# A hybrid decoder layer on one core: mLSTM row sums formed by matmuls against a two-column constant, with factors turned through DRAM and key sums taken by VectorE

## The chip, the cores and the metric

The kernel is one launch on one core of a Trainium2 chip. The core has five engines that run side by side and wait for one another through semaphores: PE (TensorE, matrix products; PEld is its weight loads), DVE (VectorE), ACT (ScalarE), POOL (GpSimd) and SP (SyncE, which here issues nearly all DMAs). Each engine works its instructions off in a fixed order, so an instruction that waits holds up all that stand behind it on its engine. The metric is the device time of the launch in microseconds (us), the median of several runs.

## The reference

The layer has 1024 tokens of width 1024: two groups of heads side by side (4 mLSTM heads of width 128, 8 attention heads), an output product, a cross attention, an MLP and norms. The change lies in the mLSTM heads. What they compute, cut from the reference:

```python
scores = jnp.einsum('bhtd,bhsd->bhts', qc, kc) * jnp.exp(dmat - m_t[..., None])
num = (jnp.einsum('bhts,bhsd->bhtd', scores, vc)
       + inter[..., None] * jnp.einsum('bhed,bhtd->bhte', C, qc))
den = scores.sum(-1) + inter * jnp.einsum('bhd,bhtd->bht', n, qc)
h = num / jnp.maximum(jnp.abs(den), jnp.exp(-m_t))[..., None]
...
C_new = decay[..., None, None] * C + jnp.einsum('bhs,bhse,bhsd->bhed', wa, vc, kc)
n_new = decay[..., None] * n + jnp.einsum('bhs,bhsd->bhd', wa, kc)
...
mh = mh * lax.rsqrt(jnp.mean(mh * mh, axis=-1, keepdims=True) + EPS)
mh = mh * ml_norm[l].astype(jnp.float32).reshape(ML_HEADS, ML_DH)
ml_out = (mh.reshape(B, S, ML_W) * jax.nn.sigmoid(ml_o.astype(jnp.float32))).astype(x.dtype)
```

So each head needs, for each token, a sum over the scores (`den`), a sum of squares of `num` over the head's 128 values, and for the second half of the sequence a matrix `C` and a vector `n` carried over from the first half.

## The kernel before

**Tiling.** Tokens lie along the free axis in two halves of 512 (`TH`); the 128 values of a head lie on the partitions. Products that need float32 accuracy are three matmuls of split operands (`mm3`, L186 to L188): `split` (L134, L135) lets ACT copy a value into a shortened type (`hi`) and DVE subtract that from the value (`lo`).

**The mLSTM stage** runs from about 85 to 366 us. For head 0 to 3, `ml_project` makes the keys (`conv_silu`: a product, a convolution over 1024-wide rows on DVE, a SiLU), one tile of attention queries and one of attention keys (`fx_project(0)`, `fx_project(1)`, which have nothing to do with the mLSTM head), the carried state (`carried`), the mLSTM queries (`conv_silu` again), the carried part of numerator and denominator (`carry`) and the output gate `og`. `ml_head` then works over two halves of tokens: for each of four blocks of keys a score product into an `sc` bank, times an exponential (ACT L587, POOL L589, DVE L590), split (L134, L135), and multiplied by the values into the bank `ov`; POOL adds the weighted scores up into `acc` (L594).

**Row sums before.** At the end of a half, `sum_cols` (L217) multiplies each 128-column piece of `acc` and of the squares `sq` by a column of ones: 8 matmuls of one column, whose results lie with tokens on the partitions, 128x4 each. Small DVE operations on 128x8 columns (L612 to L618, with a power on POOL, L204) form the factor `fac`. `to_row` (L249 to L253) transposes `fac` on PE, stores it to DRAM (`facd`) and loads it back as a row spread over 128 partitions. In L629, L630, L137, L138 `num` is multiplied by norm, factor and gate, split and stored to `mix`.

**The carried state before.** `carried` transposes the first half of the keys (L527), scales the transposed columns by a weight `wc` (L529, into `kw`), splits, multiplies by the values (L540) and sums `kw` over tokens by 4 more matmuls with the column of ones (L542).

**What sets the order.** The program is written as straight code and a generator, `ml_head`, whose tail is resumed from `ml_project` of the next head through `next(closing, None)`, so that the end of a head is issued among the products of the next one. A scheduler then fixes one order per engine when the kernel is built. Buffers come in rings: PSUM has `sc` (3 banks), `tp` (2), `mm`, `m2` and `ov` (1 each); SBUF rings `r_a` to `r_y` hold 512-wide tiles, `r_f` (the numerators) two of them. A matmul into a bank waits until the bank's last reader is done, and a write to an `r_` tile waits for the store of the tile that had the buffer before.

## Time and profile before

| | |
|---|---|
| time, median of 3 runs | 1522.53 us (1522.43 to 1523.9) |
| the profiled execution | 1523.35 us, its span 1521.6 us |
| PE busy | 1502.7 us, 99% of the span |
| DVE, ACT, POOL busy | 1100.3, 727.7, 510.1 us |
| granted TensorE clock | 0.998 over the span |
| mLSTM stage, 85 to 366 us | 281 us, a little under a fifth of the span |

Busy time is what an engine spends in instructions; a row of the timeline gives the start, the length, the engine, the line of the source and the tiles as output<-input. Matmuls are pipelined: a row's length is longer than the distance to the next row's start, and it is the distance from one start to the next that PE's time is made of.

### The profile page before, as it was taken

What the parts mean: (1) busy time and instruction counts of PE and PEld (TensorE: products, weight loads), DVE (VectorE), ACT (ScalarE), POOL (GpSimd) and SP (SyncE); (2) the same over time, 40 slices, a digit from 0 to 9 for tenths busy, and PEclk for the clock granted to TensorE, in tenths of its full rate; (3) what the DMA queues carried; (4) which work ended last, traced back from release to release, by engine and by line L of the source; (5) the groups of instructions that cost most, each with busy time, mean ns of one, the idle gap of its engine ahead of it and who ended that gap; (6) DMA issues with size and microseconds to landing.
All of it is one profiled execution on the core that took longest, in us unless ns stands there. A gap on an engine that the chain in (4) does not pass through costs nothing.

```text
span 1521.6 us, 21977 instructions
## 1 busy us (share of the span) xinstructions
PE 1502.7 (99%) x7694; PEld 1261.5 (83%) x7694; DVE 1100.3 (72%) x1743; ACT 727.7 (48%) x1360; POOL 510.1 (34%) x543
## 2 busy tenths in 40 slices
PE   9999999999999999999999999999999999999997
PEld 9988888889999788888888877778787888888887
DVE  7766676765787786944457989898887667787665
ACT  7324343334687665644443456666664621122124
POOL 1003030413364442511110034544555265663322
PEclk9999999999999999999999999999999999999999
DMA  6322223435888886843344437776678777776623
GB/s 239 109 77 87 98 100 114 135 126 157 246 244 267 260 264 230 300 131 124 119 147 157 153 134 277 247 256 242 222 252 286 291 277 276 276 270 248 239 94 111
DMA packets 122538, 299.86 MB, mean 197 GB/s; under 512 B 13614, under 2 KB 28264, under 8 KB 115516
## 3 DMA queue, kind: packets, MB, share of 16 engines
q1 hardware_dynamic: 122428, 298.46, 57.4%
q8 instruction: 60, 0.98, 0.3%
q14 instruction: 50, 0.41, 0.1%
HBM read 199.60 MB, written 98.81 MB: 196 GB/s over the span
## 4 chain that ended last, share of the span: by engine, by line
PE 93%; DVE 3%; ACT 2%; DMA 1%; issue 1%; SPq 0%; DVEq 0%; POOLq 0%; POOL 0%; ACTq 0%
PE tp L186 8%; PE tp L187 8%; PE tp L188 8%; PE m L186 6%; PE sc L186 6%; PE m L187 6%; PE m L188 6%; PE sc L187 6%; PE sc L188 6%; PE mm L186 6%; PE mm L187 6%; PE mm L188 6%; PE ov L186 2%; PE ov L187 2%; PE ov L188 2%; PE ov L801 2%
## 5 line engine op out<-in xcount | busy, mean ns | idle before, releaser
L186 PE MATMUL tp<-act,wl 128*128 128x512 f32 (+1 forms) x440 | 172.9, 393 | 1.2 <-ACT row L1396 0.7
L187 PE MATMUL tp<-act,wh 128*128 128x512 f32 (+1 forms) x440 | 172.1, 391 | 0.0
L188 PE MATMUL tp<-act,wh 128*128 128x512 f32 (+1 forms) x440 | 171.7, 391 | 0.0
L135 DVE TENSOR_TENSOR wl<-wr,wh 128x1024 fp32r<-128x1024 f32 (+2 forms) x95 | 124.5, 1311 | 22.0 <-ACT wh L134 21.4
L134 ACT ACTIVATE wh<-wr 128x1024 fp32r<-128x1024 f32 (+2 forms) x95 | 95.6, 1007 | 75.9 <-PE tp L188 34.7
L186 PE MATMUL mm<-act,wl 128*128 128x512 f32 (+1 forms) x332 | 127.5, 384 | 0.0
L188 PE MATMUL mm<-act,wh 128*128 128x512 f32 (+1 forms) x332 | 127.3, 383 | 0.0
L187 PE MATMUL mm<-act,wh 128*128 128x512 f32 (+1 forms) x332 | 127.2, 383 | 0.0
L186 PE MATMUL m<-act,wl 128*128 128x512 f32 (+1 forms) x308 | 117.7, 382 | 0.5 <-DVE wl L135 0.5
L188 PE MATMUL m<-act,wh 128*128 128x512 f32 (+1 forms) x308 | 117.7, 382 | 0.0
L187 PE MATMUL m<-act,wh 128*128 128x512 f32 (+1 forms) x308 | 117.5, 381 | 0.0
L186 PEld LDWEIGHTS tp<-act,wl 128*128 128x128 f32 x440 | 82.6, 188 | 20.6 <-ACT row L1396 1.2
L188 PEld LDWEIGHTS tp<-act,wh 128*128 128x128 f32 x440 | 82.6, 188 | 18.9
L187 PEld LDWEIGHTS tp<-act,wh 128*128 128x128 f32 x440 | 82.7, 188 | 18.5
L186 PE MATMUL sc<-act,wl 128*128 128x512 f32 (+1 forms) x248 | 97.0, 391 | 1.0 <-DVE wl L135 1.0
L188 PE MATMUL sc<-act,wh 128*128 128x512 f32 (+1 forms) x248 | 96.7, 390 | 0.0
L187 PE MATMUL sc<-act,wh 128*128 128x512 f32 (+1 forms) x248 | 96.6, 390 | 0.0
L1467 POOL TENSOR_TENSOR z<-wr 128x256 f32<-128x256 f32 x56 | 51.7, 944 | 130.6 <-DMA wr<-w_ff2q 116.8
L134 ACT ACTIVATE wh<-z 128x1024 fp32r<-128x1024 f32 (+1 forms) x54 | 55.5, 1028 | 80.8 <-POOL z L1467 58.4
L135 DVE TENSOR_TENSOR wl<-z,wh 128x1024 fp32r<-128x1024 f32 (+1 forms) x54 | 74.3, 1376 | 7.8 <-ACT wh L134 7.6
L134 ACT ACTIVATE w<-wr 128x768 fp32r<-128x768 f32 (+2 forms) x31 | 25.5, 823 | 106.2 <-PE tp L186 33.7
L188 PEld LDWEIGHTS mm<-act,wh 128*128 128x128 f32 x332 | 62.3, 188 | 12.7
(726 smaller groups left out, 4288.4 us busy)
## 6 DMA issues: line engine op xcount, KB each, us to landing
act<-right SPq DMA_DIRECT2D x49, 1024.0 KB
right<-w SPq DMA_DIRECT2D x56, 256.0 KB
wr<-w_ff2q SPq DMA_DIRECT2D x28, 512.0 KB
right<-r_d SPq DMA_DIRECT2D x49, 256.0 KB
right<-r_e SPq DMA_DIRECT2D x49, 256.0 KB
act<-fqk SPq DMA_DIRECT2D x48, 256.0 KB
wr<-w_in SPq DMA_DIRECT2D x20, 512.0 KB
wr<-w_ff SPq DMA_DIRECT2D x20, 512.0 KB
```

The lines of the kernel that those rows point to most:

```text
L134: s.activation(hi, src, AF.Copy)
L135: return v.tensor_tensor(out=lo, in0=src, in1=hi.bitcast(F32), op=ALU.subtract)
L186: nc.tensor.matmul(ps, w[1], x[0], start=first, stop=False, skip_group_check=more)
L187: nc.tensor.matmul(ps, w[0], x[1], start=False, stop=False, skip_group_check=more)
L188: nc.tensor.matmul(ps, w[0], x[0], start=False, stop=last, skip_group_check=more)
L801: nc.tensor.matmul(self.ov[:, c0:], self.fv[:, self.j], t[:, c0:], start=self.j == 0 and t is self.p[1], stop=self.last and t is self.p[0])
L1467: g.tensor_tensor(out=o, in0=x, in1=y, op=op)
```

## The change

Four parts, with the new line numbers:

1. **Sums by a two-column constant.** `sums(hf)` splits `acc` and the squares into `hi` and `lo` (2 ACT copies, 2 DVE subtractions of 128x512), and multiplies all four by a 128x2 piece of the constant `pick` (L586): columns (1, 0) for `acc`, (0, 1) for the squares. So 4 matmuls of 512 columns fill a 2x512 row in an `sc` bank; ACT copies it out (L588) and SP stores it to `sumd` in DRAM (L589).
2. **Turned through DRAM.** A load of `sumd` in another shape (L627) brings the sums to 128x8 columns. `fac` is stored (L639) and loaded twice as a row (L642), without the transpose on PE. `emc` comes by the same way from a store of `tops` instead of 8 transposes.
3. **Carried keys.** The keys are weighted before the transposes: `rels`, a row in DRAM, is loaded on all partitions (L530), exponentiated, and one `tensor_tensor_reduce` (L532) multiplies and sums for `n_`. The transposes (L536) then take the weighted keys, and the four matmuls with ones are gone.
4. **Later.** `sums(0)` is issued within the second half, after its block 1; `sums(1)`, the load of the columns and the rest follow at the resumptions of the next head, whose places move: after `carried`, after the queries' convolution, after `fx_project(1)`, after `carry`. Behind the last head the resumptions lie in the attention stage's first slots (0 and 6 instead of 1 and 11) and at tokens 2 and 5 instead of 4.

The core of the diff:

```diff
     def carried(hd, y):
...
-        s.activation(wc, gcol[:, 0:4, hd], AF.Exp, bias=m0)
-        v.tensor_scalar(out=wc, in0=wc, scalar1=0.5 * float(P) ** -0.5, scalar2=None, op0=ALU.mult)
+        yw = w2("c")
+        load(yw, rels[hd : hd + 1].broadcast_to([P, TH]))
+        s.activation(yw, yw, AF.Exp, bias=m0)
+        v.tensor_tensor_reduce(out=yw, in0=y[:, :TH], in1=yw, scale=0.5 * float(P) ** -0.5, scalar=0.0, op0=ALU.mult, op1=ALU.add, accum_out=n_)
         kt = mm() if hd else sc()
...
-            nc.tensor.transpose(kt[:, j * P : (j + 1) * P], y[:, j * P : (j + 1) * P], ident)
-        kw = w2("c")
-        v.tensor_tensor(
...
+            nc.tensor.transpose(kt[:, j * P : (j + 1) * P], yw[:, j * P : (j + 1) * P], ident)
         kh, kl = w2("d", dt=F32R), w2("e", dt=F32R)
-        split(kh, kl, kw)
+        split(kh, kl, kt)
...
-        for j in range(4):
-            nc.tensor.matmul(ps[:, 256:257], kw[:, j * P : (j + 1) * P], ones, start=j == 0, stop=j == 3, skip_group_check=True)
...
+        def sums(hf):
+            sh, sl = w2("d", dt=F32R), w2("e", dt=F32R)
+            split(sh, sl, accs_[hf])
+            sq, qh, ql = w2("c"), w2("d", dt=F32R), w2("e", dt=F32R)
+            s.activation(sq, nums[hf], AF.Square)
+            split(qh, ql, sq)
+            ps = sc()[:2]
+            for e, parts in enumerate(((sl, sh), (ql, qh))):
+                for x in parts:
+                    nc.tensor.matmul(ps, pick[:, 2 * e : 2 * e + 2], x, start=x is sl, stop=x is qh)
+            two = w2("y", p=2)
+            s.activation(two, ps, AF.Copy)
+            load(sumd[hd, :, hf * TH : hf * TH + TH], two)
...
+                if hf and d0 == 1:
+                    sums(0)
...
-            sum_cols(ps[:, 0:4], acc, 4)
-            sum_cols(ps[:, 4:8], sq, 4)
...
+        yield
+        sums(1)
+        both_ = col("dens", 16).rearrange("p (e i) -> p e i", e=2)
+        load(both_, along(sumd[hd]))
+        dens, sqs = both_[:, 0], both_[:, 1]
+        yield
+        s.activation(dens, dens, AF.Abs)
...
+        at = facd[hd : hd + 1]
+        load(along(at)[:, 0], fac)
         for hf in range(2):
             fb = w2("a")
-            at = facd[hd : hd + 1]
-            if hf == 0:
-                to_row(fb, fac, 8, at, sc)
-            else:
-                load(fb, at[:, TH:].broadcast_to([P, TH]))
+            load(fb, at[:, hf * TH : hf * TH + TH].broadcast_to([P, TH]))
             yield
```

How the order on the engines moves, at three places. **PE at the carried state of head 2** (`m_` is the bank `m2` with the transposed keys, `z_` the keys, `ov_` the scores times values of head 1, `mm_` a projection of head 2, `tp_` the carried product). Before:

```order
L188 MATMUL ov_1913<-r_d_1970,act_106 128x256
L527 MATMUL m_312_2168<-ident,z_297_2070 128x128 x3
L186 MATMUL mm_2215<-act_102,wl_2210 128x512
L187 MATMUL mm_2215<-act_103,wh_2209 128x512
L188 MATMUL mm_2215<-act_102,wh_2209 128x512
```

After those come 18 more rows into `mm_2215`, a row of 4 matmuls by `ones` and 8 rows into another bank, and only then L540. With the change:

```order
L186 MATMUL ov_1899<-r_d_1974,act_106 128x256
L187 MATMUL ov_1899<-r_e_1975,act_106 128x256
L188 MATMUL ov_1899<-r_d_1974,act_106 128x256
L536 MATMUL m_313_2132<-ident,r_c_2128 128x128 x4
L542 MATMUL tp_2141<-act_107,r_e_2138 128x256
L542 MATMUL tp_2141<-act_107,r_d_2137 128x256
```

The products that stood between the transposes and the carried product now stand ahead of both, and the transposes read `r_c`, a tile that DVE has just written, instead of the keys.

**DVE where head 3 begins** (`r_f_` are numerators: of head 2 the first half 2490 and the second 2351 in the change, 2488 and 2353 before; `r_a_` is the factor spread over the partitions, L562 is `carry` of head 3). Before:

```order
L138 SCALAR_TENSOR_TENSOR r_f_2488<-r_f_2488,r_y_2745 128x512
L629 SCALAR_TENSOR_TENSOR r_f_2353<-r_f_2353,vec,r_a_2750 128x512
L563 SCALAR_TENSOR_TENSOR r_b_2942<-z_430_2855,c_m_2752,r_c_2934 128x512
L138 SCALAR_TENSOR_TENSOR act_2597<-z_430_2855,act_2597 128x1024
L630 SCALAR_TENSOR_TENSOR r_f_2353<-w_340_2357,r_f_2353 128x512
L135 TENSOR_TENSOR wl_3347<-wr_3344,wh_3346 128x1024
L138 SCALAR_TENSOR_TENSOR r_f_2353<-r_f_2353,r_y_2790 128x512
L672 TENSOR_TENSOR w_444_2945<-m_448_2952,row 128x512
L562 TENSOR_TENSOR r_f_2941<-tp_2937,r_c_2934 128x512
```

With the change:

```order
L645 SCALAR_TENSOR_TENSOR r_f_2490<-r_f_2490,vec,r_a_2855 128x512
L135 TENSOR_TENSOR wl_3609<-wr_3606,wh_3608 128x1024
L646 SCALAR_TENSOR_TENSOR r_f_2490<-w_355_2362,r_f_2490 128x512
L135 TENSOR_TENSOR r_p_2920<-r_p_2920,r_p_2922 128x512
L645 SCALAR_TENSOR_TENSOR r_f_2351<-r_f_2351,vec,r_a_2934 128x512
L138 SCALAR_TENSOR_TENSOR r_f_2490<-r_f_2490,r_y_2929 128x512
L646 SCALAR_TENSOR_TENSOR r_f_2351<-w_355_2362,r_f_2351 128x512
L138 SCALAR_TENSOR_TENSOR r_f_2351<-r_f_2351,r_y_2949 128x512
L562 TENSOR_TENSOR r_f_2943<-tp_2939,r_c_2936 128x512
```

The final step of the first half (its L138) has moved behind the second half's wait for its factor (the second L645), and L562, which takes the buffer of the first half's numerator once that is stored, follows directly.

**ACT in the last head, from half 0 to half 1.** Before:

```order
L604 ACTIVATE r_f_3076<-ov_3011 128x512
L605 ACTIVATE r_c_3075<-ov_3011 128x512
L587 ACTIVATE r_c_3097<-r_a_3090,gcol 128x512
L134 ACTIVATE r_d_3101<-r_c_3097 128x512
L609 ACTIVATE c_dens_3007<-sc_3079 128x4
```

With the change:

```order
L621 ACTIVATE r_f_3082<-ov_3018 128x512
L134 ACTIVATE r_d_3111<-r_c_3107 128x384
L581 ACTIVATE r_c_3123<-r_f_3082 128x512
L134 ACTIVATE r_d_3119<-r_b_3019 128x512
L604 ACTIVATE r_c_3141<-r_a_3084,gcol 128x256
L134 ACTIVATE r_d_3124<-r_c_3123 128x512
L137 ACTIVATE r_b_3383<-mm_3358,rcol 128x4x64
```

Two splits (of `acc` and of the squares) have come in among the second half's operations, ahead of L137, which empties a projection's bank `mm`.

More of the change, by code (lines that the diff above doesn't have):

```diff
@@ L447, in hybrid_layer @@
     gcol = const("gcol", [P, 8, MLH])
-    emc = const("emc", [P, 8, MLH])
+    emc = const("emc", [P, MLH, 8])
+    rels = dram.tile([MLH, TH], F32, name="rels")
+    tops = dram.tile([MLH, T], F32, name="tops")
+    along = lambda x: x.rearrange("h (p i) -> p h i", i=8)
     decay = dram.tile([2, 2, GW, T], F32, name="decay")
@@ L471, in gate_rows @@
         load(rows, neg[0:MLH])
+        load(rels, rel[0:MLH, :TH])
+        load(tops, top[0:MLH])
+        load(emc, along(tops))
     def gate_cols():
-        for dst, src in ((gcol, rel), (emc, steps)):
-            tps = ov_()
-            for j in range(8):
-                nc.tensor.transpose(tps[:, j * MLH : (j + 1) * MLH], src[0:MLH, j * P : (j + 1) * P], ident[:MLH, :MLH])
-            s.activation(dst.rearrange("p a b -> p (a b)"), tps[:, : 8 * MLH], AF.Copy if dst is gcol else AF.Exp, scale=1.0 if dst is gcol else -1.0)
+        tps = ov_()
+        for j in range(8):
+            nc.tensor.transpose(tps[:, j * MLH : (j + 1) * MLH], rel[0:MLH, j * P : (j + 1) * P], ident[:MLH, :MLH])
+        s.activation(gcol.rearrange("p a b -> p (a b)"), tps[:, : 8 * MLH], AF.Copy)
+        flat = emc.rearrange("p a b -> p (a b)")
+        s.activation(flat, flat, AF.Exp, scale=-1.0)
         cut = (w4(dt=F32R)[:GW], w4(dt=F32R)[:GW])
@@ L567, in hybrid_layer @@
     facd = dram.tile([MLH, T], F32, name="facd")
+    sumd = dram.tile([MLH, 2, T], F32, name="sumd")
+    pick = const("pick", [P, 4], F32R)
+    for c0, c1, x in ((0, 1, 1.0), (1, 3, 0.0), (3, 4, 1.0)):
+        g.memset(pick[:, c0:c1].bitcast(F32), x)
     def ml_head(hd, q, k, og, num1, den1):
         fac = col("fac", 8)
-        nums = []
-        dens = col("dens", 8)
-        sqs = col("sqs", 8)
+        nums, accs_ = [], []
+        def sums(hf):
[11 more added lines that the diff above has]
+            load(sumd[hd, :, hf * TH : hf * TH + TH], two)
         for hf in range(2):
@@ L666, in ml_project @@
         yq = conv_silu(hd, *q)
+        next(closing, None)
         fx_project(1, hd)
+        next(closing, None)
         sums = carry(hd, q, yq, *state)
+        next(closing, None)
         og = w4()
@@ L1089, in hybrid_layer @@
         slot(False, 0)
-        if i in (1, 11):
+        if i in (0, 6):
             next(closing, None)
-    token_major(a["w_fv"], fv_sink, between={4: lambda: next(closing, None)})
+    token_major(a["w_fv"], fv_sink, between={t: lambda: next(closing, None) for t in (2, 5)})
     hm = act().rearrange("p a b -> p (a b)").rearrange("p (e k c) -> p e k c", e=2, k=KT)
```

23 lines of the change are left out of this document (5 added, 18 removed).

## The prediction

> **What bounds the kernel now.** First the page: busy times and the chain that ended last.
>
> ```profile
> PE 1502.7 (99%) x7694; PEld 1261.5 (83%) x7694; DVE 1100.3 (72%) x1743; ACT 727.7 (48%) x1360; POOL 510.1 (34%) x543
> PE 93%; DVE 3%; ACT 2%; DMA 1%; issue 1%; SPq 0%; DVEq 0%; POOLq 0%; POOL 0%; ACTq 0%
> ```
>
> PE is busy 1502.7 of 1521.6 us and makes 93% of the chain. Then the mLSTM stage by windows, one head each, and the start of the attention stage (columns: window, length, busy PE, PEld, DVE, ACT, POOL, granted clock, DMA share, GB/s), and the longest group of PE's waits:
>
> ```profile
> 85.00:155.00 70.00, 70.00 (x339) 58.11 (x337) 43.24 (x60) 26.15 (x42) 13.43 (x18) 1.00 0.23 76
> 155.00:226.00 71.00, 71.00 (x349) 59.19 (x349) 48.36 (x76) 26.67 (x45) 14.27 (x18) 1.00 0.29 101
> 226.00:296.00 70.00, 70.00 (x346) 58.51 (x347) 46.72 (x73) 26.18 (x45) 17.00 (x19) 1.00 0.33 108
> 296.00:366.00 70.00, 70.00 (x438) 62.56 (x437) 40.88 (x73) 26.36 (x52) 17.23 (x22) 1.00 0.50 146
> 366.00:420.00 54.00, 53.01 (x408) 50.23 (x407) 37.89 (x108) 33.41 (x93) 21.19 (x31) 1.00 0.80 234
> PE sc L734 <- ACT w L756: 2.8, 5, 1.3
> ```
>
> In the four windows of the change PE has no idle at all. So two things alone count: PE time that goes, and PE idle that comes. DVE (58% to 68% of these windows), ACT (38%) and POOL have room on average, which says nothing about waits one after the other.
>
> **What PE saves.** One 128x512 matmul, four of the column sums, the transposes of `emc` and one of `fac` (timeline of PE; what counts is start to start):
>
> ```profile
> 142.62 0.39 PE L186 MATMUL tp<-act,wl 128*128 128x512 f32 x1
> 142.85 0.95 PE L217 MATMUL sc<-ones,r_c 128*128 128x1 f32 x8
> 143.65 0.37 PE L186 MATMUL sc<-w,w 128*128 128x256 f32 x1
> 143.86 0.28 PE L187 MATMUL sc<-w,w 128*128 128x256 f32 x1
> 143.98 0.28 PE L188 MATMUL sc<-w,w 128*128 128x256 f32 x1
> ...
> 61.34 0.65 PE L477 MATMUL ov<-ident,act 4*128 4x4 f32 x8
> 61.92 0.50 PE L186 MATMUL tp<-act,wl 128*128 128x512 f32 x1
> 62.26 0.39 PE L187 MATMUL tp<-act,wh 128*128 128x512 f32 x1
> ...
> 172.56 0.28 PE L249 MATMUL sc<-ident,c_fac 128*8 128x128 f32 x1
> 172.59 0.48 PE L186 MATMUL tp<-act,wl 128*128 128x512 f32 x1
> 172.91 0.39 PE L187 MATMUL tp<-act,wh 128*128 128x512 f32 x1
> ```
>
> Four columns (8 records, two to a column) take 142.85 to 143.65, 0.80, and the matmul behind them 0.21 where its like takes 0.12: 0.89 for four. The diff removes 64 columns of `sum_cols` and 16 of `carried`: 80 x 0.22 = 17.8. The `emc` transposes take 0.58, and 0.34 instead of 0.23 behind: 0.7. Each of the four `fac` transposes takes 0.03 and 0.09 behind: 0.5. Added are 32 matmuls of 512 columns with a two-column weight. No row shows one; at the pitch of a 128-column weight (142.62 to 142.85) they cost 32 x 0.233 = 7.5. That is the value I take, since the moving operand is the same kind. If they went in two passes, as the f32 columns do, they would cost 15. The 16 key transposes stay. **Saved: 17.8 + 0.7 + 0.5 - 7.5 = 11.5 us**; 4 at the bad end.
>
> **What the other engines get.** Per half head two more splits and a copy, per head a wider exponential: about 16 x 0.63 + 8 x 0.60 + 2 = 17 us more on ACT and 16 x 0.75 = 12 on DVE. Rows for these and for the chains below (groups of the mLSTM stage, then ACT's timeline, then the trip of the factor through DRAM):
>
> ```profile
> L135 DVE TENSOR_TENSOR r_e<-r_c,r_d 128x512 fp32r<-128x512 f32 x8 | 6.0, 753 | 3.6 <-ACT r_d L134 3.6
> L629 DVE SCALAR_TENSOR_TENSOR r_f<-r_f,vec,r_a 128x512 f32<-128x512 f32 x6 | 4.5, 751 | 6.1 <-DMA r_a<-facd 6.1
> L510 DVE SCALAR_TENSOR_TENSOR z<-z,vec,z 128x1024 f32<-128x1024 f32 x21 | 27.3, 1300 | 0.1
> L614 DVE RECIPROCAL c_rd<-c_dens 128x8 f32<-128x8 f32 x3 | 0.6, 203 | 0.1
> L558 ACT ACTIVATE r_c<-r_c,c_m 128x512 f32<-128x512 f32 x4 | 2.9, 723 | 7.8 <-DMA r_c<-rows 7.8
> L204 POOL TENSOR_TENSOR c_y<-c_var,half 128x8 f32<-128x8 f32 x3 | 5.0, 1652 | 30.3 <-DVE c_var L198 30.3
> ...
> 345.53 0.47 ACT L137 ACTIVATE r_b<-mm,rcol 128x256 fp32r<-128x256 f32 x1 [1.29 <-PE sc L217]
> 346.29 0.60 ACT L604 ACTIVATE r_f<-ov 128x512 f32<-128x512 f32 x1 [0.29 <-PE ov L188]
> 349.17 0.63 ACT L134 ACTIVATE r_d<-r_c 128x512 fp32r<-128x512 f32 x1 [1.18 <-DVE r_c L590]
> 350.68 1.00 ACT L587 ACTIVATE r_c<-r_a,gcol 128x384 f32<-128x384 f32 x2
> ...
> 173.16 0.29 SPq L251 DMA_DIRECT2D facd<-r_a  x1
> 176.20 0.33 SPq L253 DMA_DIRECT2D r_a<-facd  x1
> ...
> 179.36 0.75 DVE L629 SCALAR_TENSOR_TENSOR r_f<-r_f,vec,r_a 128x512 f32<-128x512 f32 x1 [1.80 <-DMA r_a<-facd]
> ```
>
> As sums these fit under PE: 12 us of DVE over 281 leave it below 75%. In a row they need not fit. A store whose landing lets its reload go took 3.04 us (173.16 to 176.20), a load from issue to the DVE step that waited for it 3.16 (176.20 to 179.36). I take these for the new transfers too: those with 128x8 pieces have no row, and could be somewhat longer. The fused multiply and sum (L532) has none either; its nearest is L629, two full operands and a column, 0.75.
>
> **Where PE now waits.** I followed each engine's order in the changed kernel and set, against each chain, the matmuls that PE still has at 0.233 (512 wide) and 0.117 (256).
>
> *Carried state of head 2.* Before, PE had products between the key transposes and what needs them:
>
> ```profile
> 226.53 0.49 PE L527 MATMUL m<-ident,z 128*128 128x128 f32 x3
> ...
> 234.51 0.28 PE L540 MATMUL tp<-act,r_e 128*128 128x256 f32 x1
> ```
>
> 8 us lie there. Now `ov` matmuls, transposes and the carried product follow each other. The row for `yw` is loaded into a ring `r_c` whose buffer comes free only when block 2 of the half before has been split by DVE and added by POOL, some 1.3 us before PE runs out of `ov` matmuls (my count; between 0 and 2.5). Load 3.16, exponential 0.72, L532 0.75 make 4.6, so 3.3 idle ahead of L536. Behind the transposes ACT's copy 0.63 and DVE's subtraction 0.75 leave another 1.5 with the handovers ahead of L542. **4.8** (3.5 to 6). Heads 1 and 3 have 5.6 us and more of products in the same gap and stay free.
>
> *Beginning of head 3.* The matmul into the bank that L562 has to empty comes 46 matmuls of 512, 3 of 384 and 72 of 256 columns after head 2's last `pick`: 10.7 + 0.5 + 8.4 = 19.7. L562 needs: copy 0.60, store 3.04, load 3.16, Abs and five small steps 1.1, the power 1.65, four small steps 0.7, store 3.04, load 3.16, L645 0.75, the second load 3.16 and L645 0.75 (which stand ahead of the first half's last step on DVE), that step 0.75, its store 3.04, L562 itself 0.7: 25.6. **5.9** (0, where each of the six trips takes 1 us less, to 7.5, where DVE's 1.3 us splits of weights, which stand between these steps, add in). Behind L562 on DVE stand L607 and the splits of head 3's first half, so all of it passes on to PE.
>
> *Beginning of head 2*, the same chain: the convolution's 1.3 us steps stand between the small steps on DVE, so `fac` is ready some 15.5 us after the `pick`; two transfers, L645, the second load, L645 and the emptying of a projection's bank bring it to 27.0 against 104 x 0.233 + 0.9 = 25.2 of matmuls. **1.8** (0 to 4).
>
> *Last head, half 0 to 1.* The next product needs a bank emptied by the seventh of seven ACT operations in a line, 0.60 + 0.52 + 0.63 + 0.63 + 0.50 + 0.63 + 0.47 = 4.0, and a DVE step of 0.5; PE has six `ov` matmuls, four `pick` and six scores, 2.9: 1.6. At the half's end L618, the square, a split on ACT and one on DVE, 2.8 against 1.5: 1.2. The bank after that waits in the same line: 1.1. **3.9** (1.5 to 5).
>
> *Smaller ones*, by the same count: a projection's bank used again at once in heads 0 and 1, `ov`'s one bank, the bank `m2`, and ACT's Abs that waits in ACT's order for its load in the attention stage: **2.5** (0 to 5).
>
> Sum 18.9, less 11.5 saved: **7.4 more**. Against the profiled execution's 1523.35 us (span 1521.6 and 1.75 around it) that is 1530.8; the runs' median, 1522.53, lies 0.8 below that execution: **1530 us**.
>
> [...]
>
> **The rivals.**
>
> *Chains covered (0.2).* The saving stands and the transfers hide. The place is the ring `r_c` and the DRAM chain: it decides once the load of `yw` goes out 4.6 us before PE runs dry and a trip takes 2.1 us instead of 3.1, which brings head 3's chain under its 19.7. For it: PE idles nowhere in these windows today, and DVE has a third of them free. Against it: the two trips measured, and that head 2's carried state has 1.3 us, not 4.6. With 0 to 6 us of waits left: 1511 to 1517.
>
> *Half of them (0.14).* Carried state, last head and the small ones bite, the two DRAM chains do not: 11.2 waits against 11.5: 1522, no change.
>
> *The clock follows the gaps (0.14).* The end of the program shows the granted clock (third column from the end) falling once PE idles:
>
> ```profile
> 1512.00:1514.00 2.00, 0.81 (x6) 0.72 (x6) 0.46 (x4) 0.47 (x1) 0.71 (x1) 1.00 0.58 199
> 1514.00:1516.00 2.00, 1.02 (x4) 0.72 (x4) 0.77 (x3) 0.00 (x0) 0.00 (x0) 0.67 0.00 0
> 1516.00:1518.00 2.00, 0.00 (x0) 0.00 (x0) 2.00 (x4) 0.00 (x0) 0.00 (x0) 0.50 0.41 138
> ```
>
> PE is idle for half of 1512 to 1516 and the clock goes from 1.00 to 0.67 and 0.50. A gap of 3 us or more in the mLSTM stage that does the same, at two or three places with 4 us at half speed behind each, costs 2 us each on top: 1534 to 1537. It decides only if the gaps come in one piece; mine at head 2's carried state and head 3's beginning do. [...]
>
> *Two passes for the pick matmuls (0.05).* Then the change does not save what it is built to: 4 us saved, 1537. Against it: their operands are split into the shortened type, whose other matmuls run at 0.233.
>
> *Forecast (0.47):* 1526 to 1534.
>
> **How the numbers follow.** A measurement here tells about 0.2%, 3 us, from none. Slower is the forecast, the clock and the two passes: 0.66; within 0.2%: 0.14; faster: 0.20. The range takes in the upper part of the first rival and ends where the clock's cost and long chains meet: 1514 to 1540; alone the forecast has 1526 to 1534.
>
> **What would show it.** PE's L217 rows in this stage and L542's columns are gone, and 32 L586 rows stand at 0.23. PE's list of waits names DVE or ACT ahead of L536 and L542 once each, 3 and 1.5 us; a matmul of a projection behind L562 some 5 us after 320; projections in the last head 1 to 2 us. A clock under 0.95 in one window of the stage speaks for the third rival. Wrong I am if PE stays busy through the four windows: then the time is 1511 to 1514.

## The result, and the profile after

| | before | after |
|---|---|---|
| median (range) us | 1522.62 (1522.43 to 1523.9) | 1542.59 (1541.74 to 1544.67) |
| runs | 4 | 4 |
| span of the profiled execution, us | 1521.6 | 1541.0 |
| PE busy, us | 1502.7 | 1500.7 |
| PE not busy, us (span less busy) | 18.9 | 40.3 |
| mean granted clock | 0.998 | 0.990 |

The change costs 20 us: the ratio is 1.0133, with a 95% interval of 1.012 to 1.0147. The predicted 1530 has the right sign, but its range ended at 1540.

First the page of the changed kernel, with the line of busy times, and then its windows over the same stretches as before (columns as in the prediction):

```profile
PE 1500.7 (97%) x7554; PEld 1249.3 (81%) x7554; DVE 1104.2 (72%) x1751; ACT 738.8 (48%) x1376; POOL 500.6 (32%) x546
```

```profile
85.00:155.00 70.00, 69.47 (x316) 56.35 (x315) 45.13 (x63) 27.57 (x43) 10.87 (x18) 1.00 0.25 81
155.00:226.00 71.00, 70.95 (x325) 57.26 (x324) 49.00 (x76) 29.63 (x48) 12.77 (x18) 1.00 0.34 106
226.00:296.00 70.00, 64.05 (x286) 51.60 (x285) 45.33 (x71) 27.23 (x44) 12.89 (x18) 0.95 0.33 107
296.00:366.00 70.00, 63.53 (x336) 53.14 (x335) 40.63 (x67) 25.52 (x46) 13.94 (x18) 0.96 0.37 110
366.00:420.00 54.00, 43.98 (x324) 40.45 (x324) 26.95 (x80) 22.99 (x63) 14.92 (x20) 0.91 0.79 213
```

The first two heads are as full as before. In the third and the fourth window PE is idle for 6 us each, and in the last for 10, where before it had 0, 0 and 1. In the same three windows the granted clock, which stood at 1.00 before, is 0.95, 0.96 and 0.91. So two things cost time there. The list of PE's waits in the changed kernel (total, times, longest) names the idle:

```profile
PE tp L799 <- DVE r_e L135: 7.8, 1, 7.8
PE tp L186 <- DVE r_f L562: 4.9, 1, 4.9
PE m L536 <- DVE c_m L532: 4.4, 1, 4.4
...
PE tp L542 <- DVE r_e L135: 1.4, 1, 1.4
```

Three single waits are 17.1 us. L536 and L542 are the carried state of head 2, L562 the beginning of head 3, and L799 stands in the attention stage.

For what the clock costs I cut 85 to 500 us into windows of 1 us and add up PE's busy time times one less the granted clock: before 0.0 us, after 7.5. The same sum over the idle gives 3.0 before and 24.6 after. By place:

| place in the changed kernel, us | PE idle | lost to the clock |
|---|---|---|
| 226 to 238, carried state of head 2 | 5.97 | 2.13 |
| 344 to 354, beginning of head 3 | 4.94 | 1.66 |
| 360 to 367, last head | 1.43 | 1.62 |
| 370 to 375, last head | 1.40 | 0 |
| 407 to 422, attention stage | 8.36 | 2.04 |
| all others between 85 and 500 | 2.48 | 0 |

The lost clock lies inside PE's busy time. Over the whole span the loss is 0.3 us before and 7.6 after, so PE's work at full clock went from 1502.4 to 1493.1: the change saved 9.3 us of PE, as it was built to. It bought them with 21.4 us of idle and 7.3 of clock: 21.4 + 7.3 - 9.3 = 19.4, the difference of the spans.

How one such place looks, by windows of 1 us in the changed kernel (busy PE, PEld, DVE, ACT, POOL, granted clock, DMA share, GB/s):

```profile
226.00:227.00 1.00, 0.89 (x6) 0.52 (x4) 1.00 (x2) 0.00 (x0) 0.21 (x1) 1.00 0.87 340
...
228.00:229.00 1.00, 0.00 (x0) 0.00 (x0) 0.00 (x0) 0.00 (x0) 0.00 (x0) 1.00 0.36 109
...
230.00:231.00 1.00, 0.00 (x0) 0.00 (x0) 0.28 (x1) 0.69 (x1) 0.00 (x0) 0.67 0.00 0
...
235.00:236.00 1.00, 1.00 (x7) 1.00 (x6) 0.00 (x0) 0.00 (x0) 0.00 (x0) 0.50 0.00 0
...
237.00:238.00 1.00, 1.00 (x5) 0.77 (x5) 0.63 (x2) 0.63 (x2) 0.00 (x0) 0.92 0.00 0
```

PE runs dry at 227. At 228 no engine works: all wait for one load. The clock holds for some 3.3 us, falls to half at 230.3 (a mean of 0.67 in the window from 230 is a third of it at 1.00 and the rest at 0.50), and rises at 237.2 (0.92 in the window from 237), although PE is full again from 234. The full windows 235 and 236 are worth half: matmuls of 512 columns start 0.43 us apart from 235.88 to 237.16, and 0.23 apart from there on. In this trace it took 3.3 us of idle to the fall and some 3.1 of full work (234.0 to 237.2) to the rise. At the other places the clock fell after less idle, 3.11, 1.31 and 2.20 us in the 3.41 us ahead of the fall; the last section has them.

Last, the attention stage, by the timeline of the changed kernel (start, length, what; in brackets the idle before it and what ended it). L645 needs the row of factors `r_a`, one load for each half; L1111 loads 2048 KB:

```profile
397.94 0.33 SPq L642 DMA_DIRECT2D r_a<-facd  x1
...
398.87 0.53 SPq L1111 DMA_DIRECT2D act<-hmd  x1
...
403.11 0.75 DVE L645 SCALAR_TENSOR_TENSOR r_f<-r_f,vec,r_a 128x512 f32<-128x512 f32 x1 [6.20 <-DMA r_a<-facd]
403.89 0.32 SPq L642 DMA_DIRECT2D r_a<-facd  x1
...
415.99 0.75 DVE L645 SCALAR_TENSOR_TENSOR r_f<-r_f,vec,r_a 128x512 f32<-128x512 f32 x1 [7.71 <-DMA r_a<-facd]
417.40 0.69 PE L799 MATMUL tp<-ident,w 128*128 128x128 f32 x2 [7.79 <-DVE r_e L135]
```

The second load cannot go before the first L645 has freed the one buffer of `r_a`. It goes out at 403.89, behind the 2 MB, and is used at 415.99: 12.1 us. The same load before the change stood ahead of the 2 MB:

```profile
380.79 0.32 SPq L626 DMA_DIRECT2D r_a<-facd  x1
...
382.20 0.50 SPq L1094 DMA_DIRECT2D act<-hmd  x1
...
384.06 0.75 DVE L629 SCALAR_TENSOR_TENSOR r_f<-r_f,vec,r_a 128x512 f32<-128x512 f32 x1 [1.18 <-DMA r_a<-facd]
```

It took 3.3 us there. The step that ends the last head's factor starts at 371.84 before (L618) and at 393.35 after (L637). Behind the waiting L645 on DVE stands the split L135, whose result PE's L799 needs.

### The profile page after: what moved, and what is told of

It reads as the page before. It is cut to its first block, busy times and chain, and to the rows that moved or that the text cites. A ratio compares the mean times of both kernels' runs of the same rounds, so it can differ in the third digit from the quotient of the medians.

```text
span 1541.0 us, 21762 instructions
## 1 busy us (share of the span) xinstructions
PE 1500.7 (97%) x7554; PEld 1249.3 (81%) x7554; DVE 1104.2 (72%) x1751; ACT 738.8 (48%) x1376; POOL 500.6 (32%) x546
## 5 line engine op out<-in xcount | busy, mean ns | idle before, releaser
L135 DVE TENSOR_TENSOR wl<-wr,wh 128x1024 fp32r<-128x1024 f32 (+2 forms) x95 | 125.0, 1316 | 23.1 <-ACT wh L134 22.5
L135 DVE TENSOR_TENSOR wl<-z,wh 128x1024 fp32r<-128x1024 f32 (+1 forms) x54 | 74.3, 1377 | 7.9 <-ACT wh L134 7.8
```

Of the source, the lines that this page charges most:

```text
L135: return v.tensor_tensor(out=lo, in0=src, in1=hi.bitcast(F32), op=ALU.subtract)
```

## The experiments

My theory after the result: the idle has three sources of its own (the load of the key weights, the chain of transfers through DRAM, the factor load behind the 2 MB), each of the four places costs about 2 us of clock on top, and the rest is as predicted. The rivals: that the clock falls for another reason, that DVE's and ACT's extra work is what is late, or that the waits hang together, so that one removed comes back elsewhere. Times are medians in us; the ratios are to the kernel before, run with each, whose own median lay between 1522.6 and 1523.7. Gaps are given as idle + lost to the clock.

**1. Both factor loads at once.** If the second trip through DRAM is what is late at head 3 and in the attention stage, a second buffer takes it away:

```diff
+        fbs = [w2(tag) for tag in "ab"]
         for hf in range(2):
-            fb = w2("a")
-            load(fb, at[:, hf * TH : hf * TH + TH].broadcast_to([P, TH]))
+            load(fbs[hf], at[:, hf * TH : hf * TH + TH].broadcast_to([P, TH]))
+        for hf in range(2):
+            fb = fbs[hf]
             yield
```

> Edit: the second half's factor row gets a buffer of its own (ring r_b), and both factor loads are issued together, right behind the store of the factors. Everything else is the changed kernel. Theory A (long chains of transfers leave PE dry, and each long gap also costs half-clock time behind it): in the changed kernel the second load waits for the first half's step, 3 to 4 us in head 3's chain, and in the last head it then lands 12.1 us after its issue, behind a 2 MB load. So the 8.8 us of idle at 408 to 417 and its 1.8 us at half clock go, and of head 3's 5.0 + 1.6 about 5.5: 1542.6 - 16 = 1527. Rival B (the engines themselves are too late, transfers only show it): less than a third of that, 1537 or more. Rival C (the gaps go but the clock is no matter): 1542.6 - 12.7 = 1530.

Measured: 1541.36, ratio 1.012 (1.0105 to 1.0135). The time was missed, the place was not: head 3's gap went from 4.94 + 1.66 to 0.1. Head 2's carried state fell to 4.0 + 1.4, and 2.2 us of the same wait came at head 3's. But new gaps came in the last head, 4.2 + 1.6 at 357 to 367 and 6.6 + 2.7 at 373 to 390. The longest groups of PE's waits in this kernel are the attention stage's exponentials and the split that the last head's `pick` needs:

```profile
PE sc L753 <- ACT act L775: 5.8, 7, 2.0
PE sc L586 <- DVE r_e L135: 3.2, 1, 3.2
```

The buffer I took, `r_b`, also holds attention values on their way out, which suggests a collision. It can explain a part at most: PE waits 1.3 us until 382.8 and 1.6 us until 389.5 for DVE to empty a bank into `r_b`. The first gap, with the 3.2 us, lies ahead of the load into `r_b`, which goes out at 381.97. The order on all engines moved with the edit; what made the rest late is not shown.

What follows: the chain of transfers does make head 3's gap, and a second buffer at one place can cost as much at another.

**2. The 2 MB load behind the factor.**

```diff
-            load(fb, at[:, hf * TH : hf * TH + TH].broadcast_to([P, TH]))
+            last_fb[:] = [load(fb, at[:, hf * TH : hf * TH + TH].broadcast_to([P, TH]))]
...
-    load(hm.bitcast(F32), hmd)
+    with tc.issue_after(last_fb[0].ins):
+        load(hm.bitcast(F32), hmd)
```

> Edit: the 2 MB load of the cross attention's memory tokens is held until the last factor load has been issued; the two factor loads stay one after the other. Theory A: the last factor load lands in 3 to 5 us instead of 12.1, so the gap at 408 to 417 falls from 8.8 to about 1 us, and the half-clock time behind it goes: 1542.6 - 7.8 - 1.8 = 1533. The gap at head 3's beginning stays at 5 us. Rival D (it is not the 2 MB but the other 256 KB loads and stores around it that fill the queues): the load still takes 8 us or more, 1539 or more.

Measured: 1544.96, ratio 1.0148 (1.0133 to 1.0164). Timeline of this kernel:

```profile
403.08 0.32 SPq L644 DMA_DIRECT2D r_a<-facd  x1
403.49 0.38 SPq L1114 DMA_DIRECT2D act<-hmd  x1
404.47 0.32 SPq L651 DMA_DIRECT2D mix<-r_y  x1
...
408.39 0.75 DVE L647 SCALAR_TENSOR_TENSOR r_f<-r_f,vec,r_a 128x512 f32<-128x512 f32 x1 [3.22 <-DMA r_a<-facd]
...
414.05 0.63 ACT L137 ACTIVATE r_y<-r_f 128x512 fp32r<-128x512 f32 x1 [2.25 <-DMA mix<-r_y]
```

The factor load takes 5.3 us instead of 12.1, and PE's idle there goes from 8.36 to 4.95. But now the store of the first half (`mix`, 404.47) is the one behind the 2 MB: ACT's L137, which needs its buffer, starts at 414.05, 9.6 us after the issue. The collision moved from a load to a store. And a new gap of 3.75 + 2.75 came at 511 to 521, where ACT's L1007 waits 5.7 us for a load of weights (`wr` from `w_out_a`); it takes back more than the 2.9 won in the attention stage, and why that load was late was not followed. That transfers are late behind the 2 MB is borne out; that they can be cured by this order is not.

**3. The key weights loaded earlier.** The ring `r_c`, which holds `yw`, comes free late; the ring of the keys' working tiles is free long before:

```diff
-        yw = w2("c")
+        yw = z4()[:, :TH]
         load(yw, rels[hd : hd + 1].broadcast_to([P, TH]))
```

> Edit: the key weights (the row rels, then the weighted keys) lie in the convolution's buffer that is free once the keys are formed, instead of the ring r_c, so the row can be loaded some 10 us before the transposes. Theory A: the 4.4 us that PE waits for the weighted keys of head 2 go, and the half-clock time of 2.1 us behind; the 1.4 us for the split of the transposed keys stays: 1542.6 - 6.5 = 1536. Rival C (clock no matter): 1538. Rival E (head 2's wait is absorbed, what follows waits anyway for DVE): 1541 or more.

Measured: 1531.36, ratio 1.0057 (1.0036 to 1.0079), 11 us better than the change and 5 better than expected. The gap at 226 to 238 is 1.39 + 0, head 3's 2.2 + 1.6 instead of 4.94 + 1.66, the one in the attention stage 6.96 + 2.21, and the clock's loss between 85 and 500 us falls from 7.5 to 3.8. The load goes out at 221.53 instead of 225.67, so the late buffer was the cause of the first place. A new gap of 2.7 + 1.5 came at 502 to 508; over the whole span the loss falls from 7.6 to 5.3.

**4. Experiments 1 and 3 together.**

> Edit: the edits of the first and the third run together (factor loads together, key weights early). Theory A: the gains add, 1542.6 - 16 - 6.5 = 1520, about the kernel before or a little under it, with the granted clock back at 0.997 or more. Rival B: 1533 or more. Rival C: 1526.

Measured: 1537.17, ratio 1.0085 (1.0066 to 1.0104). The gap at 226 stays cured (1.60 + 0), but the last head's gaps of experiment 1 are there again: 5.8 + 4.2 at 347 to 366 and 5.9 + 3.3 at 372 to 390. The edits do not add up.

**5. The last head as before.** Heads 0 to 2 keep the new sums; in the last head each sum stands where it was, by columns, and the factor is turned by PE. The places of the resumptions stay those of the change.

```diff
+        old = hd == MLH - 1
...
+            if old:
+                s.activation(sq, nsb if hf else num, AF.Square)
+                ps = sc()
+                sum_cols(ps[:, 0:4], acc, 4)
+                sum_cols(ps[:, 4:8], sq, 4)
...
+            if old and hf == 0:
+                to_row(fb, fac, 8, at, sc)
```

> Edit: in the last head alone the row sums, the factor and its turn into a row are formed as before the change (columns by matmuls with ones, the transposes of the factors on PE); heads 0 to 2 keep the new way. Theory A, sharpened by the earlier runs: the last head's factors come 16 us after its last sums instead of 7, so its two loads and two stores fall among the attention stage's transfers, and its splits stand in ACT's line between its halves. With the old way there, the gap at 407 to 422 (8.4 idle, 2.0 at half clock) and the ones at 360 to 375 (2.8 and 1.6) go, and 16 columns less 8 matmuls of 512, 1.7 us, come back: 1542.6 - 14.8 + 1.7 = 1530. Rival F (the transfers of the attention stage delay the factors wherever they lie): 1538 or more.

Measured: 1535.24, ratio 1.0075 (1.0051 to 1.0098). The gap of 8.36 + 2.04 is gone (0.57), and of the two in the last head 1.25 + 1.71 stays. The other two stay as they were: 5.75 + 2.62 and 4.90 + 2.08. The median falls by 7.4 us and the span of the profiled execution by 8.8, which adds up: PE's idle falls by 9.7 and the clock's loss by 0.7, and 1.6 of PE's saving is given back (7.7 instead of 9.3). The attention stage gives 9.8 of it and the last head 1.5, while the clock costs 0.9 more at the two places that stay.

**6. Experiments 3 and 5 together.**

> Edit: the last head as before the change, and the key weights loaded early (the edit that gave 1531.4). Theory A: from that run's gaps go 7.0 + 2.2 at 396 to 409 and 1.9 at 359 to 369, and part of the 2.2 + 1.6 at 348 to 355, against 1.7 that come back: 1520 to 1522, the kernel before or a little under it. Rival F: 1528 or more.

Measured: 1522.16, ratio 0.9992 (0.9975 to 1.0008), as expected. It shows something of the clock as well. Windows of 1 us in this kernel:

```profile
227.00:228.00 1.00, 0.73 (x5) 0.29 (x2) 0.85 (x3) 0.75 (x2) 0.81 (x2) 1.00 0.87 193
228.00:229.00 1.00, 0.62 (x3) 0.42 (x3) 1.00 (x3) 0.28 (x1) 0.71 (x1) 1.00 0.89 342
229.00:230.00 1.00, 0.50 (x2) 0.30 (x2) 0.71 (x3) 0.61 (x2) 0.00 (x0) 1.00 0.13 47
230.00:231.00 1.00, 0.91 (x6) 0.91 (x7) 1.00 (x3) 0.33 (x1) 0.00 (x0) 0.81 0.00 0
231.00:232.00 1.00, 1.00 (x6) 0.90 (x6) 0.23 (x1) 0.20 (x2) 0.00 (x0) 0.50 0.05 16
```

PE is idle for only 1.24 us from 227 to 231, in pieces, and the clock still goes to half, for 1.67 us of loss. A second fall, 1.9 + 1.7, stands at 494 to 500. Elsewhere 1.4 us and even 2.4 us of idle in such pieces left it at 1.00 (370 to 375 in the changed kernel, 347 to 351 in experiment 9).

**7. The gap filled with matmuls that nobody needs.** This asks of the clock alone: 38 matmuls of 256 columns go into the bank of the key transposes ahead of them, in head 2, and the transposes overwrite what they leave.

```diff
+        if hd == 2:
+            w = lastw[0]
+            for _ in range(38):
+                nc.tensor.matmul(kt[:, 0:256], w[:, 256:384], w[:, 256:512], start=True, stop=True)
         for j in range(4):
```

> Edit: the changed kernel, with 38 matmuls of 256 columns added on PE just ahead of the key transposes of head 2, into the bank that these overwrite; their results are not used. They last 38 x 0.117 = 4.4 us, as long as PE waits there. Theory A (a gap costs its own length and then half-clock time): the transposes start no earlier, but the clock stays at 1.00 behind them and 2.1 us come back: 1540.5. Rival C (the clock is no matter, or PE's busy time counts as such): 1542.6 or up to 2 us more.

Measured: 1538.80, ratio 1.0092 (1.0066 to 1.0119). Windows of 1 us in this kernel:

```profile
230.00:231.00 1.00, 0.94 (x8) 0.73 (x7) 0.49 (x1) 0.48 (x1) 0.00 (x0) 1.00 0.00 0
...
235.00:236.00 1.00, 1.00 (x6) 0.80 (x5) 0.48 (x2) 1.00 (x3) 0.00 (x0) 1.00 0.00 0
```

The load is as late as ever (the transposes start at 231.27, in the change at 231.48), but the clock now stays at 1.00 where it was 0.67 and 0.50. The place costs 4.4 us of empty matmuls (38 x 0.117) and 1.74 of idle, 6.1 together, where it cost 5.97 + 2.13 = 8.1. Adding work that computes nothing gained 2.0 us at this place, so here the clock went with PE's idle. The rest of the 3.8 us came in the attention stage, 6.98 + 1.39 instead of 8.36 + 2.04.

**8. The carried keys alone.** The kernel before, with only the third part of the change, and the key weights in the early ring of experiment 3.

```diff
+        yw = z4()[:, :TH]
+        load(yw, rels[hd : hd + 1].broadcast_to([P, TH]))
+        s.activation(yw, yw, AF.Exp, bias=m0)
+        v.tensor_tensor_reduce(out=yw, in0=y[:, :TH], in1=yw, scale=0.5 * float(P) ** -0.5, scalar=0.0, op0=ALU.mult, op1=ALU.add, accum_out=n_)
...
-        for j in range(4):
-            nc.tensor.matmul(ps[:, 256:257], kw[:, j * P : (j + 1) * P], ones, start=j == 0, stop=j == 3, skip_group_check=True)
```

> Edit: the kernel before with the carried keys' part alone (weighted keys, fused sum on VectorE, no matmuls with ones in the carried state), and the row loaded early into the convolution's buffer; row sums, factors and the places of the closings as before. Theory A: 16 columns of 0.22, 3.6 us, are saved, and one wait of up to 1.4 us for the split of the transposed keys comes: 1519 to 1521, faster than both. Rival G (this part needs the others, or its split waits in each head): 1523 or more.

Measured: 1524.49, ratio 1.000 (0.9988 to 1.0013), where 1519 to 1521 was expected. PE's work at full clock falls by 2.4 us (1502.4 to 1500.0; 16 columns at 0.22 would be 3.5), and one wait for head 3's weighted keys, 2.88 + 1.67 at 294 to 302, takes them back:

```profile
PE tp L531 <- DVE c_m L527: 2.9, 1, 2.9
```

L527 is the fused multiply and sum, L531 the transposes of its result. So this part is worth nothing here by itself, even with the early load.

**9. The row sums alone, in heads 0 to 2.** Old carried keys, old last head (the edit of experiment 5). If only the two causes of experiment 6 mattered, this kernel would be near the kernel before.

```diff
-            nc.tensor.transpose(kt[:, j * P : (j + 1) * P], yw[:, j * P : (j + 1) * P], ident)
+            nc.tensor.transpose(kt[:, j * P : (j + 1) * P], y[:, j * P : (j + 1) * P], ident)
...
+        for j in range(4):
+            nc.tensor.matmul(ps[:, 256:257], kw[:, j * P : (j + 1) * P], ones, start=j == 0, stop=j == 3, skip_group_check=True)
```

> Edit: the changed kernel with two parts undone: the carried keys as before the change, and the last head's sums and factors as before; left are the row sums by the constant and the turn through DRAM in heads 0 to 2. Theory A: saved are 48 columns x 0.22 less 24 matmuls x 0.233, and 1.1 for transposes, 6 us; head 2's gap at the carried state is gone (it came with the key weights), head 3's beginning keeps its gap of 4.9 and 2.1 at half clock (it comes with the chain of transfers): 1523.3 - 6 + 7 = 1524. Rival H (head 3's gap goes too, since PE is 5 us later or earlier against the chain): 1517 to 1519, faster than before. Rival B (DVE and ACT short of time): 1530.

Measured: 1536.46, ratio 1.0091 (1.0076 to 1.0107), the largest surprise. There is no gap at the carried state (0.75 at 226 to 229), but one of 5.68 + 3.08 at 262 to 274, where head 2 begins. Timeline of this kernel (L674 is L645, L599 is L586):

```profile
243.24 0.39 PE L599 MATMUL sc<-r_d,pick 128*2 128x512 f32 x1
...
261.34 0.75 DVE L674 SCALAR_TENSOR_TENSOR r_f<-r_f,vec,r_a 128x512 f32<-128x512 f32 x1 [4.70 <-DMA r_a<-facd]
...
265.65 0.75 DVE L674 SCALAR_TENSOR_TENSOR r_f<-r_f,vec,r_a 128x512 f32<-128x512 f32 x1 [0.49 <-DMA r_a<-facd]
...
266.94 0.69 DVE L687 SCALAR_TENSOR_TENSOR r_p<-tp,row 128x512 f32<-128x512 f32 x1 [0.54 <-DMA fqk<-r_p]
...
267.68 0.80 PE L186 MATMUL tp<-act,wl 128*128 128x512 f32 x1 [5.70 <-DVE r_p L687]
```

From the last `pick` to the emptied bank the chain takes 24.4 us (243.24 to 267.63), and PE has work for 18.7 (to 261.98). In the changed kernel the same bank was emptied 25.2 us after the `pick` (242.27 to 267.48), and PE had no wait there, since it had that much work left. With the old carried keys some 6 us of a projection's products stand ahead of the carried product once more (228.5 to 234.2), that is ahead of the `pick` and not behind it. In these orders the same products cover either the key transposes or the denominators' chain, not both. This gap is 8.8 of the 18.5 us of idle and clock that the kernel has more than the kernel before. The rest, above all 2.4 + 0 at 347 to 351 (head 3's beginning), 0.9 + 1.7 at 373 to 380 and 2.8 + 1.7 at 396 to 404, was not followed.

**10. Experiment 6 with five empty matmuls** ahead of head 2's carried product, to hold the clock over that kernel's 1.24 us of idle.

```diff
+        if hd == 2:
+            w = lastw[0]
+            for _ in range(5):
+                nc.tensor.matmul(ps[:, 0:256], w[:, 256:384], w[:, 256:512], start=True, stop=True)
```

> Edit: the kernel with the last head as before and the key weights early (1522.2), with 5 matmuls of 256 columns, whose results are overwritten, ahead of head 2's carried product; the order on PE moves with them, and 12 projection matmuls of 512 columns come to stand in the same place. There the parent has 1.2 us of idle in four pieces within 3 us, and 1.7 us at half clock behind. Theory A: both go, 2.9 less 0.6 for the 5 matmuls: 1520, under the kernel before by 0.2%. Rival C: 1522.5 or more, no change to its parent.

Measured: 1526.60, ratio 1.0027 (1.0015 to 1.0038), slower than its parent and not faster. The place was cured (0.46 + 0), but the five matmuls shifted the order of the work behind them, and gaps of 1.48 at 266 to 268, 2.41 + 3.09 at 297 to 308 and 3.7 + 1.7 at 496 to 505 came. So it says nothing more on the clock.

**11. Experiments 1 and 5 together.** Experiment 1 won head 3's gap and lost as much in the last head; with the last head as before, the loss should go.

```diff
+        fbs = [w2("a")] if old else [w2(tag) for tag in "ab"]
```

> Edit: last head as before the change (the run that gave 1535.2, whose gaps were 5.75 + 2.6 at 226 to 239 and 4.9 + 2.1 at 345 to 355), and in heads 0 to 2 the two factor loads issued together into two buffers; key weights late, as in the change. Theory A (the second gap is the chain of six transfers, one of which now runs beside another): the gap at 345 goes with its clock, the one at 226 stays: 1535.2 - 7 = 1528. Rival I (a gap that goes only uncovers the next one, since DVE follows the same chain): 1533 or more.

Measured: 1527.36, ratio 1.0026 (1.0012 to 1.004). The time is the expected one, the places are so only in part. The gap at head 3's beginning is 0.59, as expected, and the last head's 1.25 + 1.71 of experiment 5 is gone. The gap at 226 to 236 stays with 4.18 + 2.52. But one of 3.07 + 2.93 at 301 to 311 is new, as the rival had it: one gap goes and another is uncovered. So the expected number came out by errors that cancel in part. Both gaps are transposes of keys that wait for their weights:

```profile
PE tp L539 <- DVE c_m L535: 3.1, 1, 3.1
PE m L539 <- DVE c_m L535: 2.8, 1, 2.8
```

**12. All three cures:** key weights early, factor loads together in heads 0 to 2, last head as before; the edits are those of experiments 3, 1 and 5, with no line of its own.

> Edit: all three together: last head as before, factor loads together in heads 0 to 2, key weights early. Its parent without the factor loads gave 1522.2, with no gap left from the chain of transfers. Theory A: nothing left for the factor loads to win, 1521 to 1523, the kernel before within 0.2%; what stays against the 8 us saved are gaps of about 1 us each at blocks' ends and in the attention stage. Rival J (the chain still costs through DVE's order): 1519 or less, faster.

Measured: 1518.88 (1517.7 to 1520.89), ratio 0.9966 (0.9952 to 0.998): 5 us less than the kernel before and 24 less than the change. Page and windows of this kernel:

```profile
PE 1495.9 (98%) x7579; PEld 1250.6 (82%) x7579; DVE 1105.3 (73%) x1749; ACT 736.1 (48%) x1373; POOL 501.6 (33%) x546
```

```profile
226.00:296.00 70.00, 68.42 (x314) 55.17 (x313) 50.95 (x78) 29.62 (x49) 18.12 (x23) 1.00 0.37 118
296.00:366.00 70.00, 69.66 (x452) 62.91 (x451) 40.24 (x74) 27.88 (x54) 16.94 (x20) 1.00 0.45 135
366.00:420.00 54.00, 51.92 (x388) 48.72 (x387) 39.98 (x114) 35.69 (x101) 22.43 (x32) 1.00 0.83 243
```

The clock is 1.00 in all three windows that had fallen; one fall of 1.7 us, with 2.0 of idle, is left at 489 to 496. Of the change's 9.3 us this kernel keeps 8.3 (work at full clock 1494.1) and idles 23.3 instead of 18.9 in all. The expected time was 1521 to 1523; the rival had 1519 or less, and its time came. Its reason is not shown. Against experiment 11 the early load closes both gaps at the key transposes. Against experiment 6 the idle at 227 to 230 is no smaller (1.58, where it was 1.24), but the clock did not fall there this time, which is 1.6 of the 3.7 us between the two profiled executions.

## Why the prediction missed

**What held.** PE was the bound, and the two things to count were PE time that goes and PE idle that comes. The `pick` matmuls run in one pass:

```profile
324.21 0.39 PE L586 MATMUL sc<-r_e,pick 128*2 128x512 f32 x1
324.44 0.39 PE L586 MATMUL sc<-r_d,pick 128*2 128x512 f32 x1
```

They stand 0.23 apart, the value taken. The place and the releaser of three waits were named as they came:

| term | predicted | idle measured | |
|---|---|---|---|
| carried state of head 2 | 4.8 (L536 3.3, L542 1.5) | 5.8 (4.4, 1.4) | named waits |
| beginning of head 3, L562 | 5.9 | 4.9 | |
| beginning of head 2 | 1.8 | 0 | 5.7 in experiment 9 |
| last head, half 0 to 1 | 3.9 | 2.8 | 1.43 + 1.40 |
| smaller ones, attention stage in them | 2.5 | 7.9 | attention stage 8.4, the rest 0.5 less than before |
| the granted clock | a rival, 0.14 | 7.3 | |
| saved by PE | 11.5 | 9.3 | |

Without the last three rows the waits are right within 3 us: 16.4 predicted, 13.5 measured. The miss by terms is 7.3 us of clock, 2.5 more idle (21.4 against 18.9 in all) and 2.2 less saved, 12.0 together; with the predicted 7.4 that is the 19.4 by which the spans differ.

**The first step that failed** is the sum's last line: it counted waits and gave the clock to a rival. The prediction wrote that the clock "decides only if the gaps come in one piece; mine at head 2's carried state and head 3's beginning do". By that sentence its own forecast held two gaps of 4.8 and 5.9 us and had to carry the clock's price with them. Forecast and rival were the same case, and I set them apart as if one could have the gaps without the price. The price was 1.6 to 2.1 us for each place, as the rival said; there were four such places, not two or three. No run shows the rival's 3 us for the least gap and 4 us at half speed: they were my estimates, and ahead of the result I had only the end of the program, with the clock at 0.67 and 0.50 from 1514 to 1518. The four falls came at places with 1.43 to 8.36 us of idle, and the clock stayed at half for 3.41 to 10.24. The condition was too narrow as well: the last head's 1.43 us of idle came in pieces and still cost 1.62 of clock. Experiment 7 shows the clock by itself: same late load, filled gap, clock at 1.00, 2.0 us back.

**The second** is the smaller ones: "ACT's Abs that waits in ACT's order for its load in the attention stage: 2.5 (0 to 5)", together with three others. The place was seen, but priced from transfers of the quiet mLSTM stage, 3.04 and 3.16, and for a wrong instruction: not the Abs was late, but L645 and its second load. The windows quoted in the prediction had the warning: a DMA share of 0.80 from 366 to 420 against 0.23 to 0.50 before it. The factor came 21.5 us later than before the change, so its second load fell behind the 2 MB. Measured: 12.1 us for the load, 8.4 of idle, 2.0 of clock. Experiment 5 takes the last head's new sums away, and the gap with them; experiment 2 moves the 2 MB, and the load takes 5.3.

**Smaller.** The load of `yw` took 4.3 us from issue to use, not 3.16, beside traffic of 340 GB/s:

```profile
225.67 0.32 SPq L530 DMA_DIRECT2D r_c<-rels  x1
...
229.97 0.72 ACT L531 ACTIVATE r_c<-r_c,c_m 128x512 f32<-128x512 f32 x1 [4.68 <-DMA r_c<-rels]
```

That is the 1.1 us by which L536 was worse. In head 3's chain, on the other hand, the small store took less than the 3.04 of the row it was priced by:

```profile
325.59 0.26 SPq L589 DMA_DIRECT2D sumd<-r_y  x1
...
326.81 0.37 SPq L627 DMA_DIRECT2D c_dens<-sumd  x1
```

The reload goes out 1.2 us after the store, and the chain from the `pick` to L562's start took 24.3 us, where the prediction had 24.9 (25.6 less L562's own 0.7). That the totals agree is in part luck. The two small stores and the load of the sums (326.81 to ACT's use at 328.69) took 4.7 us less than their rows. The steps between, the two factor loads and the end took 4.1 us more. And the last link was another than the predicted store of the numerator: L562 stands on DVE behind the second half's last step (L138), which waits for ACT's L137, and this for the store that frees the one buffer of `r_y`:

```profile
347.25 0.63 ACT L137 ACTIVATE r_y<-r_f 128x512 fp32r<-128x512 f32 x1 [5.37 <-DMA mix<-r_y]
347.91 0.69 DVE L138 SCALAR_TENSOR_TENSOR r_f<-r_f,r_y 128x512 fp32r<-128x512 f32 x1 [2.98 <-ACT r_y L137]
...
348.75 0.69 DVE L562 TENSOR_TENSOR r_f<-tp,r_c 128x512 f32<-128x512 f32 x1
```

The saving is 2.2 us short of 11.5: of it, experiment 8 places 1.1 in the carried keys (2.4 instead of 3.5). What PE spends there was not tried further and stays open.

**What no term had** is how the places hang together. Experiment 9 has the beginning of head 2 at 5.7 us, and the change itself at 0, because products that no longer cover the key transposes cover the chain behind the `pick`. Each term alone was priced by PE's work left at its place; that the work is one and the same was not seen. Among the four rivals, that of the clock had the right cause, and 1534 to 1537 as its time; with 8.4 us for the attention stage in place of the 2.5 it would have been 1540 to 1543. That this meets the measured 1542.6 is in part luck, since the other waits came out 2.9 us smaller and the saving 2.2.

## What to carry to other kernels

A gap that is forecast can carry the clock's price with it: of the five places of the changed kernel with 1.40 us or more of PE idle, four had half clock behind it, at 1.62 to 2.13 us each. That belongs in the forecast and not in another case. A chain through DRAM costs what its transfers cost at the place where it ends up, beside the loads that run there (one factor load 12.1 us behind the 2 MB, 3.3 ahead of it), and its buffers must be free there too. Where several chains are covered by the same products, price them together: moving the cover from one can uncover the other (5.7 us of idle at head 2 in experiment 9).

## What was not expected of the hardware

The clock's half state lasts well beyond the gap: at head 2's carried state 3.1 us of full work ran at 0.50, and the four places lost 1.6 to 2.1 us each. It also came with 1.24 us of idle in pieces (experiment 6, 227 to 231) and did not with 2.44 (experiment 9, 347 to 351), so the sum of idle alone does not decide.

The traces show what goes with it. In the changed kernel the half clock lasts from 230.33 to 237.16 (6.83), 349.80 to 353.21 (3.41), 363.45 to 366.87 (3.41) and 411.24 to 421.48 (10.24): 2, 1, 1 and 3 times 3.41 us, and these starts lie 35, 4 and 14 times 3.41 us apart. In experiment 9 it lasts 6.82, 3.42 and 3.40, from 267.02, 376.24 and 400.14, which lie 32 and 7 times 3.41 us apart. In the 3.41 us ahead of its four falls the changed kernel has 3.29, 3.11, 1.31 and 2.20 us of PE idle, as the profile counts it. Of its seven stretches of 3.41 us at half clock, the four after which the clock rose have 0.26, 0, 0.12 and 0 of idle, and the three followed by another have 2.30, 3.41 and 2.74. At full clock the idle of one such stretch does not decide alone either: 342.97 to 346.39 has 1.83, more than the 1.31 ahead of a fall, and full clock came behind it. Laid out from the falls of their own kernels in the same way, the 2.44 us of experiment 9 lie in two stretches, 1.27 and 1.17, and the 1.24 of experiment 6 lie in the one ahead of its fall. What else decides is not shown. A stretch of 3.41 us of full work at a clock of 0.50 costs 1.7 us, which is why so many of the losses above are 1.7.

A load of 256 KB that took 3.3 us before the change took 12.1 behind one of 2 MB, with all four compute engines idle for 5 us:

```profile
410.00:415.00 5.00, 0.00 (x0) 0.00 (x0) 0.00 (x0) 0.00 (x0) 0.00 (x0) 0.62 1.04 283
```
